# Attention of the second block: keys stacked on the partitions, a mask of 64 bf16 columns, and the projections in another order

## The chip, the cores and the metric

The kernel runs on one core of one Trainium2 chip. The metric is the device time of one launch in microseconds. In the rows, PE is the matrix engine (TensorE) and PEld its loading of weights, DVE the vector engine, ACT the scalar engine, POOL GpSimd and SP SyncE. A matmul written 128x256 sends 256 columns of the moving operand past 128 rows of weights. Names such as `kh<-pt,gcol` read "out from in".

## What is computed

Two blocks in a row, on 1024 positions of 1024 channels. The change lies in the causal attention of the second block: 8 heads, each with two score maps of 64 channels, whose difference weighs the values. The relevant lines:

```
q = rope_partial(rms_norm(q, q_norm), cos, sin) * (64 ** -0.5)      # [1024, 8 heads, 2, 64]
k = rope_partial(rms_norm(k, k_norm), cos, sin)
for blk in range(1024 // 128):                                      # a tile of 128 queries
    q0, q1 = blk * 128, (blk + 1) * 128
    sc = einsum('bqhmd,bkhmd->bhmqk', q[:, q0:q1], k[:, :q1])
    mask = (arange(q1) // 64)[None, :] <= (arange(q0, q1) // 64)[:, None]
    p = softmax(where(mask, sc, -1e30), axis=-1)
    w = p[:, :, 0] - lam * p[:, :, 1]
    outs.append(einsum('bhqk,bkhd->bqhd', w, v[:, :q1]))
o = rms_norm(concatenate(outs), subln) * (1.0 - lambda_init)
```

So in the last 128 keys of a tile only one corner is masked: the first 64 queries do not see the last 64 keys. The gate products (`w_gl2`, `w_ga2`) and the output products that stand beside the attention in the program are other matrix products of the same block.

## The kernel before

Every f32 product is made of three matmuls on operands split into a high and a low part (`mm3`, lines 174, 175, 176). The scores take two: the stationary operand holds the 64 channels of the query's high part and, in the other 64 partitions, its low part, so one matmul against `kh` (the keys' high part, written twice, once per half of the partitions) and one against `kl` give the whole product (lines 1478, 1479). Line 1481 adds the mask as a third matmul of 256 f32 columns, `ma` (ones in the first row for the first 64 queries) by `mb` (minus 2 to the 100 in its first row, for the last 64 keys).

The 8 heads are taken as 4 pairs. A pair has 8 tiles of queries in the order 0, 7, 1, 6, 2, 5, 3, 4 and two heads, so 16 units, 64 in all. A unit runs `unit_qk` (scores, maximum, exponentials), `unit_mix` (the difference of the two maps), `unit_tr` (transposes of the weights and their split into `wth` and `wtl`), `unit_pv` (the product with V) and `unit_o` (the sum of the parts). While one unit is on DVE and ACT, TensorE works on pieces that the generator `fillers` yields: projections of k, v and q (24 matmuls of 128x256 each, tile `pj`, evicted by ACT as `pc`) and gate units (24 matmuls of 128x512, tile `pg`, `tanh` on ACT into `tg`, and a DMA from POOL's queue). `pj` and `pg` share one PSUM buffer. `need` pulls fillers until a tile is there, `fill` pulls some microseconds' worth, and `done` holds back a piece whose buffers are still in use. The tiles of a pair's keys (`kh`, `kl`) and values (`V`) have one buffer each, so the keys of the next pair are not written before the last scores of this one are made.

Normalized keys are written as a tile `nr` of 512 columns with every head twice (line 1231 on), transposed by four f32 transposes (`transposed`, L1248), and evicted by one ACT (`kh`) and one DVE instruction (`kl`). `attn_out` normalizes four finished tiles of a head: DVE and POOL work, then, a unit later, four transposes (L1549), an ACT eviction `ot` and a DMA. `tg` and `ot` have a buffer of their own each. At the end of the stage `outputs_ahead` splits eight chunks `b00` to `b07` of the next stage (one ACT and one DVE instruction each), and `outputs_early` gives their products (tile `po` of 128x512) as further fillers.

The program states the order in which instructions are written, with priorities. The scheduler then sets each engine's order by them, by its own estimate of when operands are ready and by buffers coming free. Each engine runs its order strictly.

Of the kernel before, what the change touches and what calls it, by code (L numbers as in the profile page):

```python
# [11 lines left out]
F32 = mybir.dt.float32  # L12
F32R = mybir.dt.float32r
BF = mybir.dt.bfloat16
# [115 lines left out]
class Model:  # L130
# [1034 lines left out]
    def attention(self):  # L1165
# [4 lines left out]
        with self.pool("at1") as T1, self.pool("at") as T, \  # L1170
# [19 lines left out]
            nc.gpsimd.memset(mb.bitcast(F32), 0.0)  # L1190
            nc.vector.memset(ma.bitcast(F32)[0:1, 0:64], 1.0)
            nc.vector.memset(mb.bitcast(F32)[0:1, 192:256], -(2.0 ** 100))
            self.at = (T, PS, PT, PJ, ma, mb, lamn, sub)

# [24 lines left out]
            def norm_rope(ps, i, is_k):  # L1219

                d = T1.tile([128, 4, 2, 64], F32, name="nr", tag="nr", bufs=3)
# [8 lines left out]
                if is_k:  # L1230
                    self.tt(d, ps[:, :, None, :].to_broadcast([128, 4, 2, 64]),
                            ss[:, 4:8, None, None].to_broadcast([128, 4, 2, 64]), OP.mult)
# [3 lines left out]
                for j in range(2):  # L1236
# [4 lines left out]
                self.tt(d[:, :, :, 0:16], r[:, 0, :, None, :].to_broadcast([128, 4, 2, 16]),  # L1241
                        r[:, 1, :, None, :].to_broadcast([128, 4, 2, 16]), OP.add)
                return d, ss[:, 4:8]

            def transposed(d):
                pt = PT.tile([128, 4, 128], F32, name="pt", tag="pt")
                for a in range(4):
                    nc.tensor.transpose(pt[:, a], d[:, a].rearrange("p a b -> p (a b)"), self.ident)  # L1248
                return pt
# [9 lines left out]
            def gate_unit(u):  # L1259
# [9 lines left out]
                t = T.tile([128, 512], F32, name="tg", tag="tg", bufs=1)  # L1269
# [3 lines left out]
            KV = {}  # L1273
            QS = {}
            WQ = {}

            def k_tiles(p):
                wk = w2(A["w_k2"][p])
                wv = w2(A["w_v2"][p])
                yield "k", p  # L1280
                kh = T.tile([128, 4, 1024], F32R, name="kh", tag="kh")
                kl = T.tile([128, 4, 1024], F32R, name="kl", tag="kl")
                V = T.tile([128, 8, 2, 2, 128], F32R, name="V", tag="V")
                KV[p] = [kh, kl, V]
                pend = []

                def finish():
                    j, d = pend.pop(0)
                    pt = transposed(d)
                    q = slice(j * 128, j * 128 + 128)  # L1290
                    self.act(kh[:, :, q], pt, AF.Copy, scale=gcol[:, 1:2])
                    self.stt(kl[:, :, q], pt, gcol[:, 1:2], kh[:, :, q].bitcast(F32), OP.mult, OP.subtract)

                for n in range(8 + 2):
# [5 lines left out]
                    if n == 1:  # L1300
                        yield "v", p
                    if n > 1:
                        j = n - 2
                        o = []
                        yield from proj(wv, j, o)
                        ps = o[0].rearrange("p (h a) b -> p h (a b)", h=2)
                        self.split(V[:, j, :, 0], V[:, j, :, 1], ps)
                        finish()
                        yield 0.3
                        if j == 3:  # L1310
                            WQ[p] = w2(A["w_q2"][p])

            def q_tile(p, i):
# [5 lines left out]
                qs = T.tile([128, 4, 128], F32R, name="qs", tag="qs", bufs=QB)  # L1319
                self.act(qs, pt, AF.Copy, scale=gcol[:, 0:1])  # L1320
                self.stt(qs[64:128], pt[64:128], gcol[64:128, 0:1], qs[64:128].bitcast(F32),
                         OP.mult, OP.subtract)
# [7 lines left out]

# [1144 lines left out]
```

## Time and profile before

| | us |
|---|---|
| median of 3 runs | 2524.95 (2524.49 to 2526.47) |
| the profiled execution | 2524.15 |
| its span | 2522.4 |
| attention stage of the second block, about | 720 to 1460 of the span |
| busy in the whole span: PE, DVE, ACT, POOL | 2366.1, 1786.7, 1246.9, 546.1 |

The profiled execution is 0.8 us under the median, and 1.75 us of it lie outside the span. Matmuls are pipelined: a matmul's own duration (0.28 us for 128x256) is longer than the distance to the next (0.12 us), so the rate is read from the start times of a timeline and not from the mean duration. Idle time of TensorE begins only when the last long duration has ended, and so the time lost between two starts is somewhat more than the idle time shown for it.

### The profile page before, as it was taken

How to read it: one execution, taken by the hardware profiler on the slowest of the kernel's cores; microseconds unless marked ns; L12 is line 12 of the kernel's file. 1: busy time of each engine (PE TensorE's matmuls, PEld its weight loads, DVE VectorE, ACT ScalarE, POOL GpSimd, SP SyncE). 2: the span in 40 equal slices, each digit the busy share in tenths (PEclk: the TensorE clock that was granted, in tenths of full speed). 3: DMA queues.
4: the chain of work that ended last, by engine and by line, in shares of the span. 5: the costliest groups of instructions: out<-in, count | busy, mean ns of one | idle time of the engine just before them, and what ended most of it. 6: DMA issues, size and time to landing. Idle time of an engine off the chain costs nothing. (4 is left out here: it accounts for less than half of the span.)

```text
span 2522.4 us, 34498 instructions
## 1 busy us (share of the span) xinstructions
PE 2366.1 (94%) x13016; PEld 1956.4 (78%) x13016; DVE 1786.7 (71%) x3206; ACT 1246.9 (49%) x1850; POOL 546.1 (22%) x377
## 2 busy tenths in 40 slices
PE   8999989989989999899999899999988999988887
PEld 6888868777888898798898778888876777666665
DVE  9667767686876666666666744336658999988887
ACT  5344532553655455455454522124435777766664
POOL 1011114112131021021121100000002333255552
PEclk9999999999999999999999999999988999999999
DMA  6321353322111111111111456532158998999995
GB/s 222 95 76 61 112 200 113 109 70 89 63 60 46 63 46 39 51 51 38 51 51 47 146 198 218 181 137 82 70 217 290 381 372 311 367 335 337 337 334 188
DMA packets 103833, 394.29 MB, mean 156 GB/s; under 512 B 14128, under 2 KB 33072, under 8 KB 79088
## 3 DMA queue, kind: packets, MB, share of 16 engines
q1 hardware_dynamic: 85008, 335.18, 37.6%
q0 software_dynamic: 18656, 56.88, 7.2%
q8 instruction: 104, 1.70, 0.3%
q14 instruction: 65, 0.53, 0.1%
HBM read 339.07 MB, written 61.31 MB: 159 GB/s over the span
## 5 line engine op out<-in xcount | busy, mean ns | idle before, releaser
L166 DVE TENSOR_TENSOR wl<-raw,wh 128x2048 fp32r<-128x2048 f32 (+2 forms) x310 | 580.8, 1887 | 118.3 <-ACT wh L154 118.0
L154 ACT ACTIVATE wh<-raw 128x2048 fp32r<-128x2048 f32 (+2 forms) x310 | 479.7, 1557 | 286.2 <-PE pj L175 83.4
L2238 POOL DMA_INDIRECT out<-y,lsti x32 | 175.2, 5475 | 331.4 <-DVE y L162 281.5
L175 PE MATMUL pg<-wl,xh 128*96 128x512 f32 x512 | 205.4, 401 | 30.2 <-DVE wl L166 30.0
L174 PE MATMUL pj<-wh,xnh 128*128 128x256 f32 x768 | 223.0, 290 | 10.8 <-ACT pc L154 6.0
L175 PE MATMUL pj<-wl,xnh 128*128 128x256 f32 x768 | 218.1, 284 | 0.0
L176 PE MATMUL pj<-wh,xnl 128*128 128x256 f32 x768 | 217.8, 284 | 0.0
L176 PE MATMUL pg<-wh,xl 128*96 128x512 f32 x512 | 201.6, 394 | 0.0
L174 PE MATMUL pg<-wh,xh 128*96 128x512 f32 x512 | 198.2, 395 | 1.0 <-ACT wh L154 1.0
L174 PEld LDWEIGHTS pj<-wh,xnh 128*128 128x128 f32 x768 | 146.0, 190 | 14.3 <-ACT pc L154 8.1
L175 PEld LDWEIGHTS pj<-wl,xnh 128*128 128x128 f32 x768 | 146.2, 190 | 0.0
L176 PEld LDWEIGHTS pj<-wh,xnl 128*128 128x128 f32 x768 | 145.9, 190 | 0.0
L175 PEld LDWEIGHTS pg<-wl,xh 128*96 128x96 f32 x512 | 82.8, 162 | 76.5 <-DVE wl L166 44.6
L179 POOL TENSOR_TENSOR ss<-ss,mhalf 128x4 f32<-128x4 f32 (+1 forms) x68 | 73.0, 1074 | 313.7 <-DVE ss L163 219.3
L154 ACT ACTIVATE e<-sc,st,ss 128x1024 f32<-128x1024 f32 (+7 forms) x128 | 105.7, 829 | 67.3 <-DVE st L158 50.4
L174 PEld LDWEIGHTS pg<-wh,xh 128*96 128x96 f32 x512 | 82.8, 162 | 37.2 <-ACT wh L154 1.4
L174 PE MATMUL pj<-xnh,wh 128*128 128x512 f32 x256 | 103.3, 404 | 5.6 <-ACT wh L154 5.6
L176 PEld LDWEIGHTS pg<-wh,xl 128*96 128x96 f32 x512 | 83.0, 162 | 32.7
L174 PE MATMUL pg<-xnh,wh 128*128 128x512 f32 x256 | 102.9, 402 | 0.0
L175 PE MATMUL pj<-xnl,wh 128*128 128x512 f32 x256 | 102.2, 399 | 0.0
L176 PE MATMUL pg<-xnh,wl 128*128 128x512 f32 x256 | 102.1, 399 | 0.0
L176 PE MATMUL pj<-xnh,wl 128*128 128x512 f32 x256 | 101.9, 399 | 0.0
(998 smaller groups left out, 6480.8 us busy)
## 6 DMA issues: line engine op xcount, KB each, us to landing
raw<-in_w_gu SPq DMA_DIRECT2D x128, 1024.0 KB, 7.3
raw<-in_w_dn SPq DMA_DIRECT2D x64, 1024.0 KB, 9.2
raw<-in_w_out SPq DMA_DIRECT2D x16, 512.0 KB, 4.7
ta<-tg POOLq DMA_DIRECT2D x32, 256.0 KB, 2.6
t<-ta SPq DMA_DIRECT2D x14, 512.0 KB, 4.6
raw<-in_w_ga SPq DMA_DIRECT2D x12, 512.0 KB, 3.8
raw<-in_w_v SPq DMA_DIRECT2D x12, 512.0 KB, 3.4
xraw<-in_xT SPq DMA_DIRECT2D x8, 512.0 KB, 7.6
```

The costliest lines, as they stand in the source:

```text
L154: return self.nc.scalar.activation(out=out, in_=in_, func=func, **kw)
L166: return (eng or self.nc.vector).tensor_tensor(out=out, in0=a, in1=b, op=op)
L174: mm(ps, l[0], r[0], start=start, stop=False)
L175: mm(ps, l[0], r[1], start=False, stop=False)
L176: mm(ps, l[1], r[0], start=False, stop=stop)
L179: self.nc.gpsimd.tensor_tensor(out=out, in0=in_, in1=self.mhalf[:, :w], op=OP.pow)
L2238: return nc.gpsimd.indirect_dma_start(out=self.out, out_offset=bass.IndirectOffsetOnAxis(ap=u["row"], axis=0), in_=u["y"], in_offset=None, ...
```

## The change

Keys: one tile `kk` with two buffers holds the high part in one half of the partitions and the low part in the other. Which half holds which alternates with the map m. Only 256 columns are normalized and transposed (two transposes instead of four), and the eviction is two ACT and two DVE instructions of 64 partitions by 256. The query tile `qs` holds the high part and the low part as two planes of all 128 partitions, and each plane is multiplied by `kk`. The count and the shapes of the score matmuls stay. The mask: `ma` and `mb` become bf16, and `mb` has 64 columns. Its matmul covers the last 64 columns alone. `tg` and `ot` move from their own buffers into the ring of three `nr` buffers, which the normalized tiles use. Order: within a pair the last two gate units are followed by the next pair's keys, and the first query tile of that pair among them. Its values are projected after its first scores (`v_tiles`, held until unit 15's product with V), and `need(vals, p)` stands ahead of the first product with V.

```
-            ma = T.tile([128, 128], F32R, name="ma")
-            mb = T.tile([128, 384], F32R, name="mb")
-            nc.gpsimd.memset(ma.bitcast(F32), 0.0)
+            ma = T.tile([128, 128], BF, name="ma")
+            mb = T.tile([128, 64], BF, name="mb")
+            nc.vector.memset(ma, 0.0)
...
-                d = T1.tile([128, 4, 2, 64], F32, name="nr", tag="nr", bufs=3)
+                w = 1 if is_k else 2
+                d = T1.tile([128, 4, w, 64], F32, name="nr", tag="nr", bufs=3)
...
+                v = d.rearrange("p a b c -> p (a b c)")
+                n = v.shape[1] // 128
-                for a in range(4):
-                    nc.tensor.transpose(pt[:, a], d[:, a].rearrange("p a b -> p (a b)"), self.ident)
+                for a in range(n):
+                    nc.tensor.transpose(pt[:, a], v[:, 128 * a:128 * a + 128], self.ident)
...
-                t = T.tile([128, 512], F32, name="tg", tag="tg", bufs=1)
+                t = T1.tile([128, 512], F32, name="tg", tag="nr", bufs=3)
...
-                kh = T.tile([128, 4, 1024], F32R, name="kh", tag="kh")
-                kl = T.tile([128, 4, 1024], F32R, name="kl", tag="kl")
+                kk = KV[p] = [T.tile([128, 4, 1024], F32R, name="kk", tag="kk", bufs=2), None]
...
-                    self.act(kh[:, :, q], pt, AF.Copy, scale=gcol[:, 1:2])
-                    self.stt(kl[:, :, q], pt, gcol[:, 1:2], kh[:, :, q].bitcast(F32), OP.mult, OP.subtract)
+                    for m in range(2):
+                        a, b = slice(64 * m, 64 * m + 64), slice(64 - 64 * m, 128 - 64 * m)
+                        g = gcol[a, 1:2]
+                        self.act(kk[0][a, m:4:2, q], pt[a], AF.Copy, scale=g)
+                        self.stt(kk[0][b, m:4:2, q], pt[a], g, kk[0][a, m:4:2, q].bitcast(F32), OP.mult, OP.subtract)
...
+                qs = T.tile([128, 2, 4, 128], F32R, name="qs", tag="qs", bufs=QB)
+                self.act(qs[:, 0], pt, AF.Copy, scale=gcol[:, 0:1])
+                self.stt(qs[:, 1], pt, gcol[:, 0:1], qs[:, 0].bitcast(F32), OP.mult, OP.subtract)
...
                     yield from gate_unit(8 * p + 6)
                     yield from gate_unit(8 * p + 7)
+                    if p < 3:
+                        yield "q", p + 1, 0
+                        yield from k_tiles(p + 1, q_tile(p + 1, tiles[0]))
...
+                need(vals, p)
                 for g, tr in zip(G, trs):
-                    self.unit_pv(cur, g, tr, KV[p][2])
+                    self.unit_pv(cur, g, tr, KV[p][1])
...
-                nc.tensor.matmul(base[:, o:o + n], qs[:, a], kh[:, a, k0:k0 + n], start=True, stop=False)
-                nc.tensor.matmul(base[:, o:o + n], qs[:, a], kl[:, a, k0:k0 + n], start=False, stop=not last)
+                for r in range(2):
+                    nc.tensor.matmul(base[:, o:o + n], qs[:, r, a], kk[:, a, k0:k0 + n], start=r == 0,
+                                     stop=r == 1 and not last)
                 if last:
-                    nc.tensor.matmul(base[:, o + n - 256:o + n], ma, mb[:, 128:384] if i == 0 else mb[:, 0:256],
-                                     start=False, stop=True)
+                    end = 128 if i == 0 else o + n
+                    nc.tensor.matmul(base[:, end - 64:end], ma, mb, start=False, stop=True)
...
-            ot = T.tile([128, 512], F32, name="ot", tag="ot", bufs=1)
+            ot = self.at1.tile([128, 512], F32, name="ot", tag="nr", bufs=3)
```

How the order moves is shown at three places.

**The end of the first pair, TensorE**, before: among the last products of tile 2 and tile 5 with V (`po`) stand projections of the next pair (`pj`).

```order
L1523 MATMUL po<-V,wth 128x256
L1248 MATMUL pt<-ident,nr 128x128 x4
L176 MATMUL pj<-wh,xnl 128x256
L1524 MATMUL po<-V,wtl 128x256
L1523 MATMUL po<-V,wth 128x256
L1524 MATMUL po<-V,wtl 128x256
L174 MATMUL pj<-wh,xnh 128x256
```

The same place in the changed kernel:

```order
L1549 MATMUL po<-V,wth 128x256
L1252 MATMUL pt<-ident,nr 128x128 x4
L1550 MATMUL po<-V,wtl 128x256
L1549 MATMUL po<-V,wth 128x256
L1550 MATMUL po<-V,wtl 128x256
L1537 MATMUL pt<-ident,e 128x128 x4
L1503 MATMUL sc<-kk,qs 128x320 x5
```

The two projections that stood here, 48 matmuls, have moved behind the scores of tile 4. On ACT, in the same place, before: the copy `ot` of a finished tile stands alone among the exponentials.

```order
L154 ACTIVATE wth<-pt 128x128
L154 ACTIVATE e,st<-sc,st,ss 128x640
L154 ACTIVATE ot<-pt,sub 128x512
L154 ACTIVATE e,st<-sc,st,ss 128x640
L154 ACTIVATE osq<-o_7488 128x512
```

The same place on ACT in the changed kernel:

```order
L154 ACTIVATE wth<-pt 128x128
L154 ACTIVATE e,st<-sc,st,ss 128x640
L154 ACTIVATE ot<-pt,sub 128x512
L154 ACTIVATE tg<-pg 128x512
L154 ACTIVATE e,st<-sc,st,ss 128x640
L154 ACTIVATE osq<-o_7487 128x512
```

The `tanh` of the pair's last gate unit, whose products end ahead of the stretch shown on TensorE, now stands behind `ot`; before, it stood ahead of the exponentials of tile 5.

**The first scores of the second pair, TensorE**, before: that pair's values are projected by then, and a query tile follows.

```order
L176 MATMUL pj<-wh,xnl 128x256
L1478 MATMUL sc<-kh,qs 128x256
L1479 MATMUL sc<-kl,qs 128x256
L1481 MATMUL sc<-mb,ma 128x256
L1478 MATMUL sc<-kh,qs 128x256
L1479 MATMUL sc<-kl,qs 128x256
L1481 MATMUL sc<-mb,ma 128x256
L1248 MATMUL pt<-ident,nr 128x128 x4
```

The same place in the changed kernel:

```order
L176 MATMUL pj<-wh,xnl 128x256
L1252 MATMUL pt<-ident,nr 128x128 x6
L1503 MATMUL sc<-kk,qs 128x256
L174 MATMUL pj<-wh,xnh 128x256
L175 MATMUL pj<-wl,xnh 128x256
L176 MATMUL pj<-wh,xnl 128x256
```

The first scores now follow directly on the transposes of the query tile, and the projections of values stand behind them.

**The end of the last pair, TensorE**, before: output products `po` (operands `b00` to `b07`) stand among the scores of the last units.

```order
L1479 MATMUL sc<-kl,qs 128x512
L1481 MATMUL sc<-mb,ma 128x256
L175 MATMUL po<-b05l,wh 128x512
L176 MATMUL po<-b05h,wl 128x512
L1478 MATMUL sc<-kh,qs 128x320
L1479 MATMUL sc<-kl,qs 128x320
L1478 MATMUL sc<-kh,qs 128x320
L1479 MATMUL sc<-kl,qs 128x320
L1481 MATMUL sc<-mb,ma 128x256
L174 MATMUL po<-b06h,wh 128x512
```

The scores of tile 4 in the last pair, in the changed kernel:

```order
L1508 MATMUL sc<-mb,ma 128x64
L1503 MATMUL sc<-kk,qs 128x320 x4
L1508 LDWEIGHTS ma
L1508 MATMUL sc<-mb,ma 128x64
L1537 MATMUL pt<-ident,e 128x128 x5
L1549 MATMUL po<-V,wth 128x256
L1575 MATMUL pt<-ident,o_13352 128x128 x4
L1550 MATMUL po<-V,wtl 128x256
L1549 MATMUL po<-V,wth 128x256
```

From the transposes of a query tile to the first output product there are now only instructions of the last four units; the output products begin three units later, and two of their four groups stand behind the last transposes `pt<-ident,o`.

## Rows read from the trace of the kernel before

**Rows 1.** Windows: length; busy us (count) PE, PEld, DVE, ACT, POOL; PEclk, DMA share, GB/s.

```profile
720.00:1460.00 740.00, 703.00 (x4760) 644.42 (x4758) 478.13 (x1207) 363.60 (x748) 121.25 (x144) 0.99 0.17 57
1100.00:1130.00 30.00, 29.96 (x253) 29.72 (x254) 21.57 (x53) 18.80 (x38) 5.37 (x5) 1.00 0.25 80
849.00:880.00 31.00, 28.54 (x182) 25.56 (x182) 19.99 (x45) 15.46 (x31) 2.70 (x4) 1.00 0.18 60
880.00:893.40 13.40, 9.42 (x55) 8.22 (x54) 10.40 (x31) 6.64 (x15) 1.62 (x2) 0.87 0.01 1
1232.00:1248.00 16.00, 11.83 (x87) 10.78 (x86) 11.44 (x34) 7.51 (x17) 2.31 (x2) 0.99 0.07 28
1405.40:1431.30 25.90, 19.53 (x98) 14.49 (x97) 23.00 (x43) 16.56 (x27) 2.67 (x3) 0.95 0.55 181
```

**Rows 2.** Waits of TensorE from 720 to 1460: us in total, times, longest.

```profile
PE sc L1478 <- ACT e L154: 10.4, 8, 1.9
PE pt L1511 <- DVE e L158: 7.4, 3, 2.5
```

**Rows 3.** Timeline of TensorE at the first pair end: start us, duration, instruction.

```profile
849.65 0.40 PE L176 MATMUL pg<-xnh,wl 128*128 128x512 f32 x1
851.93 0.45 PE L1478 MATMUL sc<-kh,qs 128*128 128x384 f32 x1 [1.89 <-ACT e L154]
...
880.02 0.31 PE L1478 MATMUL sc<-kh,qs 128*128 128x320 f32 x1
...
882.28 0.27 PE L1524 MATMUL po<-V,wtl 128*128 128x256 f32 x1
883.69 0.50 PE L1478 MATMUL sc<-kh,qs 128*128 128x512 f32 x1 [1.14 <-ACT e L154]
...
885.77 0.28 PE L1481 MATMUL sc<-mb,ma 128*128 128x256 f32 x1
888.50 0.76 PE L1511 MATMUL pt<-ident,e 128*128 128x128 f32 x5 [2.45 <-DVE e L158]
...
893.34 0.28 PE L174 MATMUL pj<-wh,xnh 128*128 128x256 f32 x1
```

**Rows 4.** Groups by line and shape, 715 to 1470: busy us, mean ns.

```profile
L1248 PE MATMUL pt<-ident,nr 128*128 128x128 f32 x256 | 38.4, 272 | 0.1
L1481 PE MATMUL sc<-mb,ma 128*128 128x256 f32 x128 | 36.4, 285 | 0.0
L158 DVE SCALAR_TENSOR_TENSOR kl<-pt,gcol,kh 128x512 fp32r<-128x512 f32 x32 | 24.0, 749 | 11.0 <-ACT kh L154 10.9
L154 ACT ACTIVATE qs<-pt,gcol 128x512 fp32r<-128x512 f32 x32 | 21.9, 685 | 2.8 <-PE pt L1248 2.6
L166 DVE TENSOR_TENSOR V<-pc,V 128x256 fp32r<-128x256 f32 x32 | 13.6, 426 | 1.6 <-ACT V L154 1.4
```

**Rows 5.** Timeline of TensorE: a mask matmul, and the four transposes of a key tile.

```profile
847.55 0.28 PE L1481 MATMUL sc<-mb,ma 128*128 128x256 f32 x1
847.67 0.34 PE L1478 MATMUL sc<-kh,qs 128*128 128x384 f32 x1
...
925.76 0.60 PE L1248 MATMUL pt<-ident,nr 128*128 128x128 f32 x4
926.12 0.36 PE L175 MATMUL pj<-wl,xnh 128*128 128x256 f32 x1
926.32 0.28 PE L176 MATMUL pj<-wh,xnl 128*128 128x256 f32 x1
```

**Rows 6.** Timeline of TensorE where bf16 matmuls stand before f32 ones.

```profile
1817.82 0.18 PE L2088 MATMUL prk<-cacc,one 128*128 128x32 bf16 x1
1817.84 0.47 PE L175 MATMUL pq<-wcq1l,xh 128*128 128x512 f32 x1
1818.15 0.39 PE L176 MATMUL pq<-wcq1h,xl 128*128 128x512 f32 x1
1818.38 0.39 PE L174 MATMUL pq<-wcq2h,xh 128*128 128x512 f32 x1
```

More of the change, by code (lines that the diff above doesn't have):

```diff
@@ L1273, in attention, with k_tiles @@
             KV = {}
+            vals = set()
             QS = {}
             WQ = {}
[L1277 to L1280, printed above, removed]
-                kh = T.tile([128, 4, 1024], F32R, name="kh", tag="kh")
-                kl = T.tile([128, 4, 1024], F32R, name="kl", tag="kl")
-                V = T.tile([128, 8, 2, 2, 128], F32R, name="V", tag="V")
-                KV[p] = [kh, kl, V]
+            def k_tiles(p, q=None):
+                wk = WK.pop(p)
+                kk = KV[p] = [T.tile([128, 4, 1024], F32R, name="kk", tag="kk", bufs=2), None]
                 pend = []
@@ L1299, in k_tiles, with v_tiles @@
                         pend.append((n, d))
-                    if n == 1:
-                        yield "v", p
+                    if n == (1 if q else 4):
+                        WQ[p] = w2(A["w_q2"][p])
+                    if n == 6 and q:
+                        yield from upto(q)
                     if n > 1:
[L1303 to L1307, printed above, removed]
-                        finish()
-                        yield 0.3
-                        if j == 3:
-                            WQ[p] = w2(A["w_q2"][p])
+                        finish()
+                        yield 0.2
+                if q:
+                    yield from q
+            def v_tiles(p, q=()):
+                wv = WV.pop(p)
+                V = KV[p][1] = T.tile([128, 8, 2, 2, 128], F32R, name="V", tag="V")
+                for j in range(8):
+                    o = []
+                    yield from proj(wv, j, o)
+                    ps = o[0].rearrange("p (h a) b -> p h (a b)", h=2)
+                    self.split(V[:, j, :, 0], V[:, j, :, 1], ps)
+                    if j == 0:
+                        yield from q
+                    if j == 7:
+                        vals.add(p)
+                    yield 0.1
             def q_tile(p, i):
@@ L1381, in attention, with need @@
             tail, early = [], []
-            def need(p, i):
+            def need(what, key):
                 alone[0] = True
                 n = 0
-                while (p, i) not in QS:
+                while key not in what:
                     if step() is None:
@@ L1396, in attention, with queries @@
             o4 = {}
-            done.update({("k", 0), ("v", 0)})
-            def queries(p, u):
-                for m in range(8):
-                    t = m + 1 - QB
-                    if m == 7 or t < 0 or 4 * (t // 2) + 2 + t % 2 <= u:
-                        done.add(("q", p, m))
-            queries(0, 0)
-            need(0, 7)
+            def queries(u):
+                for m in range(32):
+                    t = m - QB
+                    if t < 0 or 4 * (t // 2) + 2 + t % 2 <= u:
+                        done.add(("q", *divmod(m, 8)))
+            queries(0)
+            need(QS, (0, 7))
             cur = self.unit_qk(units[0], QS, KV)
@@ L1439, in attention @@
                     tail.append(self.attn_out(acc[0], acc[1], 2 * p + hh, k))
-                if nxt is None and n + 1 < len(units):
+                if n % 16 == 15:
                     done.add(("v", p + 1))
-                    queries(p + 1, 0)
-                    q = units[n + 1]
-                    need(q[0], q[1])
-                    nxt = self.unit_qk(q, QS, KV)
-                    fill(1.3)
-                    self.unit_mix(nxt)
                 cur = nxt
```

62 lines of the change are left out of this document (34 added, 28 removed).

## The prediction

> **What bounds the kernel now.** I read the busy time by window first, because the whole-span shares mix stages. Between 720 and 1460 us of the span, where all the changed code runs, TensorE is busy 703 of 740 us, while DVE has 478 and ACT 364 [rows 1]. In a stretch with a filler beside each unit, such as 1100 to 1130, it is busy 29.96 of 30 us at full clock, and DVE is idle for more than a quarter of the time. So in those stretches only TensorE work that disappears shortens the kernel; a shorter DVE or ACT instruction is worth nothing there. What TensorE loses lies at the pair ends and in the tail. The waits name them [rows 2]: scores wait for the exponentials of the unit that holds their PSUM buffer (10.4 us in 8 waits), and transposes for the mixed map `e` (7.4 us in 3 waits, one per pair end). The timeline of the first pair end shows the places [rows 3]: the last gate matmul starts at 849.65 and the next scores at 851.93, which is 2.28 us, against the 0.23 us that a 128x512 matmul takes in a stream [rows 6], so 2.05 us are lost. From the scores of tile 4 at 880.02 to the next projection at 893.34 no filler stands on TensorE at all: 13.3 us. With the start distances of the full clock the work there is 16 score matmuls of 0.148 us, 4 of 0.232, six masks and 17 products with V of 0.12, and nine transposes of 0.11: 7.0 us. So 6.3 us are lost, in waits of 1.3 (882.28 to 883.69) and 2.6 us (885.77 to 888.50) and in a clock of 0.87 over the stretch [rows 1, 3]. The third pair end, 1232 to 1248, repeats it with 4.2 us of idle time, against 4.0 here [rows 1]. In the tail, 1405.4 to 1431.3, it is DVE that is busy 23.0 of 25.9 us: eight splits of `b00` to `b07` lie among the last units, and TensorE works only 19.5 [rows 1].
>
> **Transposes.** Each of 32 key tiles loses two of its four. A group of four takes from 925.76 to 926.12, and the matmul behind it 0.20 instead of 0.12, together 0.44 us or 0.11 each [rows 5]. There are 256 transposes of this line, 128 of them for keys [rows 4]; 64 go, nearly all in full stretches: 64 x 0.11 = 7.0 us less. Nothing hides this gain; it is TensorE time in stretches that TensorE sets. It shrinks only where a key tile comes to lie in a stretch that waits, so its bounds are 5 and 7.
>
> **The mask.** 128 matmuls of 256 columns, at 0.12 us from start to start [rows 4, 5], become 128 of 64 columns in bf16. The trace has no such matmul followed by scores. The nearest rows are bf16 matmuls of 32 columns [rows 6]: the last one takes 0.02 us to the next start, but the f32 matmul behind it takes 0.31 us (1817.84 to 1818.15) where its neighbour takes 0.23. The 0.08 us given back fits its successor's f32 weights not being hidden behind so short a matmul. So the mask costs 0.02 + 0.08 = 0.10 to 0.105, and saves 0.013 each: 1.7 us. If the successor gives nothing back, it saves some 0.09 each, 11.5 us. I take 1.7, since behind each mask stands an f32 matmul with other weights, as in these rows. The Trainium skill, "TensorE: Matmul & The Clock Gate", section "Back-to-back issue gap", gives some 60 cycles, 25 ns, for 1 to 64 columns, with the remark that a real stream is set by the weight load as well as the matmul. By the first alone the mask would save 12 us, an estimate from that page; this trace shows the second half of the rule in the 0.31 us.
>
> **Evictions and buffers off the path.** The key eviction on DVE, 0.749 us, becomes two instructions; the nearest row of 256 elements is 0.426 [rows 4], so +0.10 us, and the normalizing of a key tile is halved, which is more. ACT's two pieces likewise cost some 0.1 us more than one. In full stretches DVE and ACT have 8 and 11 of 30 us free [rows 1], which hides it; if that cover were gone it would be below 0.2 us for each of 32 key tiles, 6 us. The query's second eviction covers twice the partitions with the same number of elements, no change. The memsets leave POOL for DVE ahead of the first keys: 0 to 0.5 us less at the start; I take 0.3.
>
> **The first pair end.** `tg` now shares a ring with `ot` and the normalized tiles, and on ACT the last gate's `tg` stands behind an `ot` that waits for a finished head. Until then that gate holds the one PSUM buffer in which a projection could start. The order shows what follows: two groups of projections, 48 matmuls, leave the stretch ahead of tile 4's scores; 48 x 0.12 = 5.7 us. The stretch 849 to 880 has 20.0 us of DVE work in 31 [rows 1], so without these fillers it can shrink to 25.3 us and DVE still has room. The extra waiting is between 0 (units follow each other as now) and 5.7 us (none of the stretch is shortened). I take 2: its DVE work and the chain of a unit leave slack, and the waits shown there are 2.05 us. The stretch without fillers behind it stays as it is.
>
> **The other two pair ends.** There the gates stand later, and a query projection stands ahead of the scores which now wait 2.05 us for the exponentials, so this wait goes: -2.05 each. The last units stay without fillers, with the loss of today.
>
> **Scores ahead of values.** At each of three pair ends the next pair's first scores come directly behind the transposes of their query tile, instead of some projections later. TensorE runs its order strictly, so the projections of values behind them are queued behind a wait for the eviction on ACT, 0.685 us [rows 4], plus the transposes' own way into PSUM. That is about 1 us, once for tile 0 and once for tile 7, where two evictions of values stand ahead on ACT. I take 2 us for a pair end, 6 in all; the bounds are 0 (the scheduler's order happens to leave enough work in between) and 3.5.
>
> **The tail.** In the last pair the gates come later, and so do the splits, which reuse the space of the operand of the gates. The 24 output products `po` that stand among the last units today leave the stretch that DVE sets [rows 1]. They save nothing there, since DVE's 23 us of work remain, and are done afterwards instead: 24 x 0.232 = 5.6 us, less some 0.5 us of slack, +5.1. The bounds are 0 and 7; two whole groups behind the last transposes cost nothing, being full work wherever they stand.
>
> **Sum.** -7.0 - 1.7 - 0.3 of gains; +2 at the first pair end, -4.1 at the other two, +6 for scores ahead of values, +5.1 in the tail: 0.0. I lower this by 1 us, for two smaller waits of a projection for an eviction ahead of tile 4's scores (the idle time of 849 to 880 is 2.5 us, some 0.5 beyond the wait for the exponentials), where no projection stands any more. On the profiled 2524.15 that is 2523.15; the median of the runs lies 0.8 above that execution, which makes 2523.95. Between the two I take **2523.5 us**.
>
> **Rivals.** *The pair ends fill.* The keys no longer wait for a free buffer; if gates and keys meet the last units in time at the second and third end, their 6.3 us each go as well, and the values' projections cover the first scores: -7.0 - 2.0 - 4.1 - 12.6 + 2 + 2 in the tail gives 2502; with half of it, 2513. For it: nothing but PSUM and the ring holds the fillers back there. Against it: the last units still stand without fillers in the order. Chance 0.20.
>
> *The mask at its full price.* With 11.5 instead of 1.7 us: 2513.7. For it: 0.02 us between bf16 matmuls. Against it: the 0.31 us behind the last one. Chance 0.12.
>
> *A longer stretch without fillers, at the low clock: slower.* After the wait of 2.6 us the clock falls today, and the granted share over 880 to 893.4 is 0.87 [rows 1, 3]; that is the level of 1.2 GHz for a part of it. At the first pair end the bare stretch gets longer by the work of some two units, and the tail gets a bare stretch of four units. If the 7 us of matmuls in each, at half the clock, take 14 in the chain of the units, where some 3 are hidden by DVE, the two cost 2 x 4 us more, 2532; it decides when more than half of these matmuls run at the low level. Against it: at 1232 to 1248 the same pattern runs at 0.99. Chance 0.21.
>
> *The order moves work without a change of the limit*: values later and keys earlier, each beside the other's place; transposes alone count, with nothing lost: 2516 to 2521. Chance 0.04.
>
> **How the numbers follow.** The forecast, 2519 to 2529, has 0.43. A measurement tells some 0.2%, 5 us, from no change: below 2519.9 is faster, above 2530 slower. Faster: 0.20 + 0.11 + 0.02 + 0.03 from the forecast's lower edge, 0.36. Slower: 0.20 + 0.02 from its upper edge, 0.22. Same: 0.42. The range from 2512 to 2533 leaves out the full first rival (0.11) and the worse half of the slower one (0.08).
>
> **What would show it.** Right: transposes of `nr` fall from 256 to 192, the mask's start distance to the next f32 start stays near 0.10; waits of TensorE at the first pair end and at the scores of tiles 0 and 7 about as long in sum as those that go; no output product between the last units, and a tail some 5 us longer. Wrong: a distance of 0.03 behind the mask; pair ends with over 29 of 30 us busy; or a clock below 0.8 in the bare stretches.

## The result and the profile after

| | before | changed |
|---|---|---|
| median of the runs, us | 2524.72 (2523.57 to 2526.47) | 2544.47 (2540.87 to 2546.52) |
| ratio | 1 | 1.0076, 95% interval 1.0059 to 1.0094 |
| span of the profiled execution, us | 2522.4 | 2543.7 |

The change makes the kernel 0.76% slower, about 19.7 us. That lies outside the range of the prediction. The windows of the changed kernel (length; busy us and count of PE, PEld, DVE, ACT, POOL; PEclk, DMA share, GB/s) answer to [rows 1]:

```profile
720.00:1460.00 740.00, 692.78 (x4643) 618.57 (x4641) 468.26 (x1232) 368.65 (x779) 119.79 (x138) 0.97 0.15 52
905.00:946.00 41.00, 36.25 (x287) 33.47 (x285) 29.29 (x83) 22.22 (x51) 9.21 (x9) 1.00 0.10 33
1417.00:1443.20 26.20, 15.68 (x76) 12.36 (x75) 22.03 (x43) 17.31 (x28) 3.11 (x3) 0.69 0.48 159
```

TensorE is busy 10 us less in the same 740 us, and DVE and ACT are far from full there. Two stretches stand out. Behind the first pair end, where the next pair's keys, values and first scores stand (905 to 946), TensorE has 4.75 idle us at full clock. In the last pair, from the last gate matmul to the first output product (1417 to 1443.2), it works 15.7 of 26.2 us at a granted clock of 0.69. Before, output products stood in that place from 1407.8 on, so the row 1405.4 to 1431.3 of [rows 1] was not a bare stretch.

The waits of TensorE from 720 to 1490 (us in total, times, longest) answer to [rows 2]:

```profile
PE sc L1503 <- ACT e L154: 10.5, 6, 3.6
PE pt L1537 <- DVE e L158: 8.4, 4, 2.5
PE sc L1503 <- ACT qs L154: 7.1, 10, 1.1
PE pj L174 <- ACT pc L154: 5.7, 5, 2.9
PE pt L1575 <- DVE st L158: 2.5, 3, 0.8
```

The waits that the change was to remove are of the same size in sum as before, 10.5 against 10.4 us and 8.4 against 7.4. But the wait of scores for the exponentials `e` has moved. The first line is the kernel before up to 1405, the other two are the changed kernel, 720 to 1410 and 1410 to 1490:

```profile
PE sc L1478 <- ACT e L154: 10.0, 7, 1.9
PE sc L1503 <- ACT e L154: 4.2, 4, 1.3
PE sc L1503 <- ACT e L154: 6.3, 2, 3.6
```

At the three pair ends 5.8 us are gone, and in the last pair 6.3 have come (0.4 before). New are the waits of scores for the query's eviction (`qs`, 7.1 us in 10 waits) and of the transposes L1575 of finished heads for their sums `st`.

To see where the 20 us lie, I read four landmarks from each timeline: the start of the 26th of the 32 mask matmuls of each pair (tile 3 of the pair), then the start of the last transpose `pt<-ident,o`, then the first matmul on the operands `b10` of the next stage. Between the first four lies one cycle of a pair each, and every cycle has the same work.

| kernel | first landmark | three cycles | to the last transpose | to the next stage |
|---|---|---|---|---|
| before | 870.8 | 179.0, 180.0, 177.7 | 52.3 | 68.3 |
| changed | 866.6 | 181.3, 181.1, 181.5 | 53.2 | 84.5 |

So -4.2 at the start, +7.2 in the cycles, +0.9 and +16.2 behind them: 20.1 us. (The first landmark lies anywhere from 866.6 to 873.7 in the kernels below, with little order in it, so the start is not read further.) The columns are used for every run below.

The largest part, behind the last transposes, is plain in the timeline of TensorE (start us, duration, instruction, idle time before it):

```profile
1463.03 1.08 PE L1575 MATMUL pt<-ident,o 128*128 128x128 f32 x4 [4.57 <-DVE o L166]
1463.77 0.78 PE L174 MATMUL po<-b00h,wh 128*128 128x512 f32 x1
...
1472.18 0.51 PE L174 MATMUL po<-b00h,wh 128*128 128x512 f32 x1 [0.78 <-DVE t L158]
...
1478.87 0.50 PE L174 MATMUL pj<-b00h,wh 128*128 128x512 f32 x1 [0.84 <-DVE t L158]
```

Two groups of output products (`po`, 24 matmuls each) start only after the last transposes, and the next stage's `pj` at 1478.87; before, all four groups were done by then and `pj` started at 1459.93. Of the 15.1 us from 1463.77 to 1478.87, the 48 matmuls are 11.1 at their distance of 0.232; about 2 are the two waits for `t`, and the rest is the lower clock behind the wait of 4.57 us (start distances of 0.43 instead of 0.23 up to 1467.75).

### The profile page after: what moved, and what is told of

It reads as the page before. It is cut to its first block, busy times and chain, and to the rows that moved or that the text cites. A ratio compares the mean times of both kernels' runs of the same rounds, so it can differ in the third digit from the quotient of the medians.

```text
span 2543.7 us, 34452 instructions
## 1 busy us (share of the span) xinstructions
PE 2368.9 (93%) x12952; PEld 1939.7 (76%) x12952; DVE 1781.9 (70%) x3240; ACT 1251.9 (49%) x1882; POOL 548.2 (22%) x375
## 5 line engine op out<-in xcount | busy, mean ns | idle before, releaser
L2264 POOL DMA_INDIRECT out<-y,lsti x32 | 175.2, 5475 | 331.5 <-DVE y L162 281.3
L1503 PE MATMUL sc<-kk,qs 128*128 128x512 f32 (+4 forms) x384 | 98.7, 371 | 18.6 <-ACT e L154 10.5
```

Source lines behind the costliest of these rows:

```text
L1503: nc.tensor.matmul(base[:, o:o + n], qs[:, r, a], kk[:, a, k0:k0 + n], start=r == 0, stop=r == 1 and not last)
L2264: return nc.gpsimd.indirect_dma_start(out=self.out, out_offset=bass.IndirectOffsetOnAxis(ap=u["row"], axis=0), in_=u["y"], in_offset=None, ...
```

## The experiments

| run | kernel | ratio to before, 95% interval | median, us |
|---|---|---|---|
| e1 | before, mask alone | 0.9982 (0.9973 to 0.9992) | 2521.7 |
| e2 | before, stacked keys alone | 0.9995 (0.9986 to 1.0005) | 2526.7 |
| e3 | before, `tg` and `ot` in the ring alone | 1.0087 (1.0060 to 1.0113) | 2547.9 |
| e4 | changed, values first | 1.0035 (1.0021 to 1.0050) | 2537.8 |
| e5 | before, `tg` alone in the ring | 1.0002 (0.9992 to 1.0012) | 2527.6 |
| e6 | before, `ot` alone in the ring | 1.0084 (1.0067 to 1.0101) | 2549.6 |
| e7 | changed, `ot` in the buffer named `e11` | 1.0115 (1.0098 to 1.0132) | 2557.8 |
| e8 | before, mask and keys | 0.9950 (0.9933 to 0.9967) | 2516.4 |
| e9 | changed, `tg` and `ot` in own buffers | 1.0053 (1.0035 to 1.0072) | 2540.5 |
| e10 | e9, values first | 0.9999 (0.9989 to 1.0008) | 2528.3 |
| e11 | e8, two query tiles held | 0.9948 (0.9930 to 0.9966) | 2513.7 |
| e12 | e6, `t` out of the ring | 1.0028 (1.0019 to 1.0038) | 2533.6 |
| e13 | changed, `t` out of the ring | 1.0045 (1.0028 to 1.0062) | 2540.0 |
| e14 | e13, values first | 1.0008 (0.9997 to 1.0019) | 2530.5 |

The ratio is to the kernel before on the same chip (its median was 2526.5 to 2528.6 there). It differs from the quotient of the medians by up to 0.1%, and medians of runs on different chips are compared by their ratios below.

**e1, the mask alone.**

```
+            ma = T.tile([128, 128], BF, name="ma")
+            mb = T.tile([128, 64], BF, name="mb")
...
+                    end = 128 if i == 0 else o + n
+                    nc.tensor.matmul(base[:, end - 64:end], ma, mb, start=False, stop=True)
```

> The kernel before with the mask of 64 bf16 columns alone. Theory A (a short matmul gives its gain back, since the f32 weights behind it are not hidden): no change, 2523 to 2526 us, and 0.12 us from the start of the last score matmul's successor to the next f32 start as before. Rival (the prediction's full price, 0.09 us for each of 128): 2513. Rival (the weights' own load of the bf16 mask costs time): 2528 or more.

It is 0.18% faster, 4.6 us; none of the three was right. The mask's own matmul explains about a quarter of it. In the changed kernel the timeline of TensorE shows what becomes of it:

```profile
846.44 0.20 PE L1508 MATMUL sc<-mb,ma 128*128 128x64 bf16 x1
846.48 0.36 PE L1549 MATMUL po<-V,wth 128*128 128x256 f32 x1
846.68 0.28 PE L1550 MATMUL po<-V,wtl 128*128 128x256 f32 x1
846.80 0.28 PE L1549 MATMUL po<-V,wth 128*128 128x256 f32 x1
```

0.04 us to the next start, but that f32 matmul then takes 0.20 instead of 0.12. Of the masks of e1 117 can be read so, and the distance behind them is 39 ns. Ahead of a score or another product (89 of them) the next matmul takes some 80 ns more, in sum about the 118 ns of before [rows 5]: nothing is saved. Ahead of a transpose (28 of them) it is different. The same place before and in e1:

```profile
780.28 0.28 PE L1481 MATMUL sc<-mb,ma 128*128 128x256 f32 x1
780.40 0.27 PE L1511 MATMUL pt<-ident,e 128*128 128x128 f32 x1
780.43 0.36 PE L174 MATMUL pj<-wh,xnh 128*128 128x256 f32 x1
780.63 0.29 PE L175 MATMUL pj<-wl,xnh 128*128 128x256 f32 x1
...
780.28 0.20 PE L1482 MATMUL sc<-mb,ma 128*128 128x64 bf16 x1
780.32 0.31 PE L1511 MATMUL pt<-ident,e 128*128 128x128 f32 x1
780.38 0.36 PE L174 MATMUL pj<-wh,xnh 128*128 128x256 f32 x1
780.59 0.28 PE L175 MATMUL pj<-wl,xnh 128*128 128x256 f32 x1
```

Here the transpose gives back only some 35 ns, and the group is about 45 ns shorter (0.35 to 0.30 us). With 28 such places that is 1.3 us, less some 0.3 for the 3 ns ahead of the products: about 1 us. The cycles fall to 176.3, 178.2 and 176.6 us, 5.6 in sum, and the rest of that lies in the order that follows. The waits of transposes for `e` fall from 7.4 to 1.7 us, while waits of products for `wtl`, 6.1 us, are new; four matmuls fewer stand between the second and the third `tanh` of a pair (12.8 to 11.9 us), which shows that the order moved and not where time was saved. I did not test which of the moves counts.

**e2, the stacked keys alone.**

```
-                kh = T.tile([128, 4, 1024], F32R, name="kh", tag="kh")
-                kl = T.tile([128, 4, 1024], F32R, name="kl", tag="kl")
+                kk = T.tile([128, 4, 1024], F32R, name="kk", tag="kk")
...
+                    for m in range(2):
...
+                        self.act(kk[a, m:4:2, q], pt[a], AF.Copy, scale=g)
+                        self.stt(kk[b, m:4:2, q], pt[a], g, kk[a, m:4:2, q].bitcast(F32), OP.mult, OP.subtract)
```

> The kernel before with stacked keys alone (one buffer, two transposes of a key tile, two evictions on ACT and on DVE with 64 partitions each, the order as it was). Theory A (64 transposes less on a full TensorE, evictions hidden): 7 us less, 2517 to 2520. Rival (the split evictions, 0.47 and 0.48 us twice instead of 0.69 and 0.75 once, hold the PSUM of the transposes and cost more than is saved): 2525 or more.

No difference that can be told from none; the time is the rival's, but the evictions are not seen to hold back the transposes in its trace (waits of L1250 for the evictions do not occur there). The transposes' price was right: a group of two costs 0.221 us with what it adds to the next matmul, one of four 0.439, over 32 key tiles 7.0 us. But the cycles are 178.2, 178.7, 178.6 and the stretch to the last transpose is 54.2, so nearly all of it is given back in waits: new are those of gate units for `tg` (4.6 us in 8 waits) and of products for `wtl` (3.0 in 8). With the mask it is not: e8 is 5 us (medians) to 8 us (ratios) below e1.

**e3, e5 and e6, the ring.** Before with both, with `tg`, and with `ot` in the ring:

```
-                t = T.tile([128, 512], F32, name="tg", tag="tg", bufs=1)
+                t = T1.tile([128, 512], F32, name="tg", tag="nr", bufs=3)
...
-            ot = T.tile([128, 512], F32, name="ot", tag="ot", bufs=1)
+            ot = self.at1.tile([128, 512], F32, name="ot", tag="nr", bufs=3)
```

> The kernel before with tg and ot in the ring of the nr tiles alone. Theory A (the shared ring is what takes the fillers from the first pair end): 4 to 10 us more, with a bare stretch on TensorE ahead of the scores of tile 4 in the first pair. Rival (the ring does nothing by itself, the order of the fillers does it): 2523 to 2526.

> The kernel before with tg alone in the ring of the nr tiles, ot in its own buffer. Theory A (the loss comes from tg and ot taking turns in one ring, so that the tanh of the last gate stands behind the copy of a finished head): as before, 2523 to 2528 us, the last gate of a pair evicted within 2 us of its last matmul. Rival (the ring of three is too small for one more user): about half of the 21 us of both, 2533 to 2540.

> The kernel before with ot alone in the ring of the nr tiles, tg in its own buffer. Theory A (both together are needed for the loss): as before, 2523 to 2528 us. Rival (the ring of three is too small): 2533 to 2540, here by nr tiles that wait for a copy to be stored.

e3 costs 22 us, more than twice the upper end of its theory: a loss as large as that of the change can be had by two lines that touch no work at all. e5 is free. e6 costs as much as both, more than either expectation. So the theory that `tg` and `ot` must meet fell. In e3 the last `tanh` of each pair comes 21 to 32 us after its matmul, in e6 within 0.8, and the total is the same: on this kernel the late gate costs nothing beside `ot`. The tiles of a ring are handed out in the order in which the program asks for them. A `tg` is made and stored soon after its gate; an `ot` waits for a head to be finished, and whoever asks behind it waits too. What both runs share is the end of the stage: 85.3 and 85.5 us behind the last transpose instead of 68.3. In e6 the DMA issues of SyncE show why (start us, duration, instruction):

```profile
1443.76 4.22 SPq L1596 DMA_DIRECT2D raw<-ob  x2
1448.15 25.22 SPq L1577 DMA_DIRECT2D t<-ta  x4
1473.43 0.89 SPq L1609 DMA_DIRECT2D t<-ta  x2
```

and before:

```profile
1434.76 0.33 SPq L1576 DMA_DIRECT2D t<-ta  x1
1435.26 1.47 SPq L1595 DMA_DIRECT2D raw<-ob  x2
1437.13 0.79 SPq L1608 DMA_DIRECT2D t<-ta  x2
```

The loads of `t`, the factor of the output products, take their buffers from the same ring. Now four of them are drawn out over 25 us, up to 1473. Before, the last one of that line went out at 1434.76, and the queue was on to the next stage's loads (L1608) by 1438. The waits of SyncE say what holds them, in e6 and in the changed kernel (us in total, times, longest):

```profile
SPq L1577 <- DMA ob<-ot: 23.4, 3, 15.0
SPq L1602 <- DMA ob<-ot: 18.7, 3, 7.0
```

They wait for `ot` to be stored. The kernel before has no such wait.

**e12 and e13, `t` out of the ring.** e12 is e6 with this line, e13 the changed kernel with it (there the tag is `to`, and two query tiles are held, for room):

```
-                t = T.tile([128, 512], F32, name="t", tag="nr", bufs=3)
+                t = self.at[0].tile([128, 512], F32, name="t", tag="ot", bufs=1)
```

> The kernel before with ot in the ring of the nr tiles, and the tile t of the output products, which was in that ring, in the buffer that ot had. Theory B (at the end of the stage the loads of t wait in SyncE's queue for the ring that ot holds, with weight loads behind them): some 10 to 13 us of the 23 go, 2535 to 2540. Rival (the whole loss is the nr tiles waiting for ot at the pair ends): 2546 to 2550. Rival (it is t alone): 2524 to 2530.

> The changed kernel with one thing undone: the tile t of the output products has a buffer of its own, while tg and ot stay in the ring (two query tiles held instead of three make the room). Theory C (two losses lie side by side: about 16 us behind the last transposes of finished heads, because t waits for ot in the ring, and some 5 us in each cycle of a pair against the kernel before with mask and keys): the stretch from those transposes to the first product of the next stage falls from 84.5 to about 69 us, the cycles stay at 181, total 2527 to 2532. Rival (in the changed kernel the tail is late because the last gates are late, whatever the ring): 2538 or more.

In e12 the loads are issued from 1442 on, the stretch behind the last transpose falls from 85.5 to 68.9 us, and 14 to 17 of the 21 to 23 us go, somewhat more than its theory had. What is left, 6 to 7 us, lies in the cycles (181.6, 183.7, 179.0 against 179.0, 180.0, 177.7). That key and query tiles wait for `ot` accounts for 1.3 us of it in the waits (`nr` for the store of `ot`, 2 times); the rest is not shown.

In e13, on the changed kernel, the same line gives back only half of the stretch, 84.5 to 76.6, with the cycles as they were; the ratio falls by 0.31%, 7.8 us. One group of output products still starts behind the last transposes. The last `tanh` runs at 1444.1, and the first product, whose tile is in the same PSUM buffer, starts at 1445.5. But `t` has one buffer here instead of three, and its loads now wait for the store of the product before them:

```profile
SPq L1602 <- DMA t<-t: 18.4, 3, 6.8
```

e12 has one buffer too, with the `tanh` at 1411.4, and loses nothing by it there. So the one buffer by itself is not the rest of the loss; the late gate, alone or together with it, is what the order of starts suggests, and no run separates the two. The time is the rival's (2538 or more), the stretch lies between theory and rival: the ring is one cause of the tail, and the late gate as the other is argued, not shown.

**e4, e9, e10 and e14, the order.** e4 and e14 put the next pair's values ahead of its first scores; e9 and e10 give `tg` and `ot` their own buffers again, with two query tiles held instead of three.

```
...
+                if nxt is None and n + 1 < len(units):
+                    queries(n + 1)
+                    need(QS, (q[0], q[1]))
+                    need(vals, p + 1)
+                    nxt = self.unit_qk(q, QS, KV)
...
-            QB = 3
+            QB = 2
```

> The changed kernel with the next pair's values projected ahead of its first scores again (the scores behind the last product of the pair before). Theory A (the waits of the first scores for the query's eviction cost 3.4 us at each of three pair ends, and the delayed gates cost the tail): 2530 to 2536. Rival (these waits only change place, the pair end loses as much elsewhere): 2541 to 2546.

> The changed kernel with tg and ot in buffers of their own, as before; to make room, two query tiles are held instead of three. Theory B (ot in the ring is the loss, the rest of the change is worth the mask's and the keys' gain less about 7 us for the values last): 2520 to 2526 us, two groups of projections back ahead of the scores of tile 4 in the first pair, and the last gate of a pair evicted within 2 us. Rival (the order loses by itself, ring or not): 2532 or more.

> As the run before, with the next pair's values projected ahead of its first scores. Theory B: some 6 us less than that run, as with the shared ring, so 2514 to 2519, near the kernel before with mask and keys alone (2516.4). Rival (gates ahead of keys and the second buffer of the keys gain by themselves): under 2512.

> As the run before, with values ahead of the next pair's scores. Theory C: cycles of 179 to 180 and a stretch of about 69 us, 2521 to 2525. Rival (the last gates set the tail): 2532 or more.

| kernel | three cycles | to the last transpose | to the next stage |
|---|---|---|---|
| e4 | 179.9, 179.4, 180.2 | 52.6 | 83.7 |
| e9 | 179.0, 183.9, 184.1 | 53.8 | 72.8 |
| e10 | 180.3, 179.3, 180.9 | 53.9 | 72.4 |
| e13 | 181.3, 181.2, 181.6 | 54.4 | 76.6 |
| e14 | 179.1, 179.6, 179.3 | 52.5 | 78.3 |
| e8 | 176.3, 175.2, 176.6 | 54.3 | 68.8 |
| e11 | 176.2, 175.3, 176.6 | 54.2 | 68.5 |

Values first returns 6 to 10 us in e4 (6.6 by the medians, taken on two chips; 0.41% by the ratios), 9.5 in e14 and 12.2 in e10: the scores ahead of values are a loss of their own. Of these three runs none met its theory's time: e4 came out between theory and rival, e10 9 us above its theory, and e14 had the cycles that it was to have and a stretch of 78.3 instead of 69. e9 is the surprise. With the ring out of the way it is still 13 us slower than before, and my theory said it would not be; its last gates are evicted within 0.8 us, as expected. Its waits:

```profile
PE pj L174 <- ACT pc L154: 17.8, 10, 3.0
PE pt L1252 <- DVE kk L158: 8.8, 6, 2.7
PE pt L1537 <- DVE e L158: 5.3, 3, 2.5
PE sc L1503 <- ACT e L154: 2.4, 4, 1.3
```

Scores wait for exponentials 2.4 us instead of 10.4, and `pt` for `e` 5.3 instead of 7.4: here the keys do fill the pair end, as they were meant to. But projections now wait 17.8 us for the eviction of the one before them and key transposes 8.8 us for the eviction of a key tile. The stretch behind, where eight key tiles and the values stand without attention units between them, waits for ACT and DVE. The wait has moved, it is not gone. The control e11 shows that the two query tiles cost nothing in the old order (its expectation is below), and e13, with two tiles and the changed kernel's order, has the changed kernel's cycles to within 0.1 us. The ring and the order do not add: e3 costs 22 us on the kernel before, taking the ring out of the changed kernel (e9) returns 4 to 6.

**e7, `ot` in another shared buffer** (one named `e11`, not the run e11)**.**

```
-            ot = self.at1.tile([128, 512], F32, name="ot", tag="nr", bufs=3)
+            ot = T.tile([128, 512], F32, name="ot", tag="e11", bufs=1)
```

> The changed kernel with ot in the buffer of the second map's exponentials of up to 512 keys (e11, which its square uses already), tg still in the ring; all else as changed. Theory A: the 16 to 25 us between the last gate matmul of a pair and its tanh go, and with them most of the loss: 2520 to 2526 us, the mask's and the keys' gains less some 3 us at each pair end for the scores ahead of values. Rival (the order with values last is the larger part): 2535 to 2544. A second rival (ot in e11 makes exponentials wait for a store): 2530 or more, with waits of e for ot's DMA.

Worse than all, as the second rival had it: cycles of 185 to 188 us, and 66.4 to the last transpose. The squares `osq` of this buffer wait for the store of `ot` on ACT, 8.1 us in 4 waits; no such wait of the exponentials shows, so the wait that is shown is a part of the loss. It says nothing on the order.

**e8 and e11, what is left when the order and the ring stay.**

> The kernel before with the mask and the stacked keys, the order and the buffers of tg and ot as they were. Theory A (the gains add up): -4.5 and -1 of the two alone, 2518 to 2522 us. Rival (the keys' evictions come into the way when TensorE is quicker): 2523 to 2527.

> The control for the two: the kernel before with mask and stacked keys, and two query tiles held instead of three. Theory B: the third query tile matters little, within 3 us of 2516.4. Rival: query tiles come late, 2522 or more, and the two runs above are to be read against that.

Both are 0.5% faster than the kernel before, and beat both kernels; they can't be told apart. e8 is 1.6 us better than the best of its theory: the gains more than add up. The waits of e11, in the columns used above:

```profile
PE pt L1515 <- DVE e L158: 7.4, 3, 2.5
PE sc L1482 <- ACT e L154: 6.4, 8, 1.4
PE pt L1553 <- DVE o L166: 3.7, 2, 2.3
PE pj L174 <- ACT pc L154: 2.8, 1, 2.8
```

The pair ends still wait (7.4 and 6.4 us), and nothing new has come. Against e8 the changed kernel has +5.0, +5.9 and +4.9 in the three cycles, 14.6 behind them and -2.2 ahead: 28.2 us, the price of order and ring together. The cycles' part lies behind the pair ends. There e8 has no wait at all (columns as in the windows above, to be held against the row 905 to 946):

```profile
895.00:945.00 50.00, 50.00 (x423) 49.75 (x423) 33.84 (x96) 29.03 (x63) 13.98 (x15) 1.00 0.19 59
```

## Why the prediction was wrong

Mask and keys were put at -8.7 us and bring 10 to 13 (e8): that half holds, though by another way. All the rest, order and ring, was put at +7.7 (-0.3 + 2 - 4.1 + 6 + 5.1 - 1) and costs 28. Two steps failed, of about the same size: in the tail, that whole groups of output products cost nothing wherever they stand, and behind the pair ends, that the stretch of keys, values and first scores stays full but for the scores' own waits.

- **Transposes, -7.0.** The price was right (439 to 221 ns for each of 32 key tiles). That nothing hides the gain was wrong: alone it is within the noise (e2), and with the mask 5 to 8 us of it come out (e8 against e1).
- **Mask, -1.7.** Ahead of products 121 ns against 118, so not even the 13 ns of the forecast; ahead of transposes some 45 ns are saved, at 28 of 117 places, about 1 us in all. So the size is nearly right, by another split than the 13 ns for each. The full price of the second rival is out. The Trainium skill, "TensorE: Matmul & The Clock Gate", section "Back-to-back issue gap", has about 25 ns for so few columns and says that in a stream the weight load sets the distance as well; the trace has 39 ns, and the 82 ns behind it fit the second half of that. That the mask brings 4.6 us, most of it by another order (e1), was in none of the cases.
- **Evictions.** A key tile's two pieces take 0.97 us on DVE where one took 0.749, 0.22 more instead of 0.10; in the changed kernel transposes of keys wait for them 0.8 us in all.
- **The first pair end, +2.** The mechanism was there: `tg` stands behind `ot`, as the ACT timeline of the changed kernel shows.

```profile
886.61 0.69 ACT L154 ACTIVATE ot<-pt,sub 128x512 f32<-128x512 f32 x1 [1.58 <-PE pt L1575]
887.20 0.59 ACT L154 ACTIVATE tg<-pg 128x512 f32<-128x512 f32 x1
```

The last gate matmul of that pair ended at 861.1. Its `tanh` comes 26 us later, where it came 0.8 us after its matmul before. (The matmul at 849.65, which the prediction calls the last gate matmul, is that of an earlier gate unit; the pair's last one stood at 868.4.) But I saw it at one pair end only. It is at all four, 26, 16, 16 and 25 us. In "the other two pair ends" I let the gates stand later and the rest as it was. The extra waiting did not come: TensorE's waits sum to 6.8 us from 836 to 905, against 6.5 from 836 to 900 before. What came is a longer time at the lower clock level: a granted clock of 0.93 over 836 to 905 against 0.97 over 840 to 900 is some 10 us at half the clock instead of 4, which costs up to 3 us (an estimate).
- **The other pair ends, -4.1.** The mechanism held, the size did not. At the second pair end the waits of the bare stretch are 0.5, 1.5, 2.6 and 1.3 us from start to start, 5.9 in sum, where the kernel before lost 2.05, 0.7, 1.3, 2.6 and 0.85, 7.5. At the third they are 6.0 where 6.7 were lost. So 1.6 and 0.7 us were gained instead of 2.05 each.
- **Scores ahead of values, +6.** The places and the size of this term were right. At the second pair end:

```profile
1108.43 0.84 PE L1252 MATMUL pt<-ident,nr 128*128 128x128 f32 x6
1110.05 0.39 PE L1503 MATMUL sc<-kk,qs 128*128 128x256 f32 x1 [0.78 <-ACT qs L154]
...
1118.38 0.49 PE L1252 MATMUL pt<-ident,nr 128*128 128x128 f32 x3
1119.99 0.73 PE L1503 MATMUL sc<-kk,qs 128*128 128x512 f32 x2 [1.12 <-ACT qs L154]
```

From these starts 0.96 and 1.28 us are lost (1108.43 to 1110.05 less six transposes, 1118.38 to 1119.99 less three), 2.2 for a pair end, 6.7 in all. What failed is that the prediction has no term for the rest of this stretch. TensorE's waits from 1085 to 1127 (us in total, times, longest):

```profile
PE sc L1503 <- ACT qs L154: 1.9, 2, 1.1
PE pt L1575 <- DVE st L158: 0.8, 1, 0.8
PE pj L174 <- ACT pc L154: 0.6, 1, 0.6
```

So projections wait for the eviction of the one before them, and the transposes of finished heads for their sums. Behind the first and the third pair end the waits of the same stretch sum to 4.5 and 4.0 us; here they are 3.3, in all 11.8, and somewhat more between starts. e8 has none there, the kernel before a fraction of a us. With values first (e4, e10, e14) 6 to 12 us come back.
- **The tail, +5.1.** This step failed by its reason: "two whole groups behind the last transposes cost nothing, being full work wherever they stand". Before, all four groups stood ahead of the last transposes and filled the waits there. Moved behind, they are 48 x 0.232 = 11.1 us ahead of the next stage, and the waits they had filled are empty: 6.3 us of scores for exponentials in the last pair, at a clock of 0.69. It measures +17.1, of which 16.2 behind the last transpose. That `t` takes its buffers from the same ring as `ot`, and that its loads stand in SyncE's queue, was not seen; on the kernel before with `ot` in the ring this is 16 us (e12), on the changed kernel 8 (e13).
- **The rivals.** The slower one had the direction, and its sign came: a granted clock of 0.69, below the 0.8 named as a sign of being wrong, over the bare stretch of the last pair. The argument against it was a misreading. The row 1232 to 1248 ends where the wait of 2.45 us ends, and the clock falls just then: over 1248 to 1253 of the kernel before it is 0.69, as at the first pair end. As the main cause the clock is out all the same. The mean granted clock of the whole execution is 0.976 in the changed kernel (2543.7 us) and 0.978 in e8 (2514.0 us); that is some 11 us more at half the clock, which can cost at most half of it, 6 of the 28 us (an estimate from these four numbers). The first rival is out for the changed kernel; e9 shows its first half, pair ends that fill, and that it pays nothing.

The forecast thus had the places of the waits that it named. It left out those of the stretch behind each pair end, took full work in the tail as free, and summed the terms as if they were independent.

What stays open: which moves of the order make most of the mask's 4.6 us; how the late gate and the one buffer of `t` share the tail of e13; and which part of the order (gates ahead of keys, the second buffer of the keys, the first query among them) makes the remaining 4 us for each cycle, and 4 behind them, between e10 and e11.

## What to carry to other kernels

Before a tile moves into a shared ring, list everyone who takes a buffer from it, in the order of the program, DMA loads included: the ring is handed out in that order, and one user who is finished late (a copy of a normalized head) holds up all who ask behind it, on queues that seem to have nothing to do with it. Work that fills waits is worth the wait it fills: moved behind the last wait it costs its full length, however dense it is there. A row of a window says something of a clock only if the window reaches past the wait after which the clock falls. And of a change with several parts, run the parts: here two of four were worth 0.5%, and the other two cost 1.1%.

## What was not expected of the hardware

A bf16 matmul of 64 columns between f32 matmuls is 39 ns to the next start. It makes a next f32 product of 256 to 512 columns some 80 ns longer, together about as long as the f32 mask of 256 columns (118 ns), but a next f32 transpose of 128 columns only 35 ns (e1). And an eviction of 64 partitions by 256 took no less time than one of 128 partitions by 256 (columns: busy us, mean ns, idle time before; the DVE rows are two different operations, the ACT rows the same one):

```profile
L158 DVE SCALAR_TENSOR_TENSOR kk<-pt,gcol,kk 64x256 fp32r<-64x256 f32 x64 | 30.9, 483 | 4.9 <-ACT kk L154 2.9
L154 ACT ACTIVATE kk<-pt,gcol 64x256 fp32r<-64x256 f32 x64 | 29.7, 469 | 22.2 <-DVE kk L158 10.9 <-PE pt L1252 10.3
L166 DVE TENSOR_TENSOR V<-pc,V 128x256 fp32r<-128x256 f32 x32 | 13.0, 422 | 22.6 <-ACT V L154 22.3
L154 ACT ACTIVATE V<-pc 128x256 fp32r<-128x256 f32 x32 | 12.7, 415 | 8.1 <-PE po L1550 7.6
```

The pieces take 0.48 and 0.47 us against the 0.43 of [rows 4], so the two pieces of a key tile take 0.97 and 0.94 us where one instruction of 128 partitions by 512 took 0.749 on DVE and, for a query tile, 0.685 on ACT [rows 4]. The prediction had put a piece at 0.43.
